# A two-layer hybrid encoder: the start of the program and the two token mixers rearranged

## The chip, the cores and the metric

The kernel runs on one core of one Trainium2 chip. The metric is the device time of one execution in microseconds. An execution of the kernel before takes 1383.24 us (median of three runs, 1381.23 to 1383.26). The five engines of the core are named as in the profile: PE is TensorE's matmul, PEld its weight load, DVE is VectorE, ACT is ScalarE, POOL is GpSimd, and SP is SyncE, which issues nearly all weight transfers here.

## The reference

A trunk of two layers over 256 tokens of width 1024, in fp32. Each layer has a token mixer and a channel mixer, each followed by a LayerNorm over the residual.

```python
def hybrid_mixer(x, ...):
    z = einsum('bsd,de->bse', x, w_in)
    cb, cc, ch, c_q, c_kv, k_r, lg, lx = split(z)
    y_conv = cb * dwconv3(cc * ch)                     # 256 channels
    y_mla  = mla(c_q, c_kv, k_r)                       # 8 heads of 64, low-rank q and kv
    y_lru  = griffin_recurrent(lg, lx)                 # 256 channels
    y = concatenate([rms_norm(y_conv), rms_norm(y_mla), rms_norm(y_lru)])
    return einsum('bse,ed->bsd', y, w_out)

def rglru_scan(x, w_a, b_a, w_i, b_i, lam, reverse):   # x: depthwise conv of 4 taps of lx
    rec = sigmoid(ga)                                  # ga, gi: block-diagonal products of x
    inp = sigmoid(gi)
    log_a = -8 * rec * softplus(-lam)
    a = exp(log_a)
    u = sqrt(-expm1(2 * log_a)) * (inp * x)
    h[t] = a[t] * h[t-1] + u[t]                        # forward, and backward with other weights
```

The first layer's channel mixer is a dense SwiGLU (3584 wide); the second's is eight SwiGLU experts of the same width, two of them for each token.

## The kernel before

The program is straight-line code in a schedule written by hand: each engine runs its instructions in the order in which the code emits them. The stages follow one another: the input LayerNorm with the transposes of x (`boundary(0)`, to about 28 us), mixer 0 (to about 125 us), `boundary(1)`, the dense channel mixer (150 to 380 us), `boundary(2)`, mixer 1 (391 to 492 us), `boundary(3)` with the router, and the experts (from about 512 us to the end).

Weights come as tiles of 1 MB (two pieces of 128 x 1024) through a ring of seven tiles. SP issues each transfer in one fixed order and waits there until the ring slot is free. `ahead` makes of a piece the two parts `hi` (rounded, by ACT at line 178 or, for the pieces in `HI_POOL`, by POOL at line 176) and `lo` (the rest, by DVE at line 185), some four pieces before `take` hands it to PE. A product of two such pairs is three matmuls (line 104). The first two pieces of a mixer are used raw, in fp32: their products go to `first` (line 330) as soon as parts of x are transposed (line 342) and copied out (lines 394, 396).

In a mixer PE runs the projections of x in the order `zq`, `zq`, gates, `zq`, gates, `zkv`, `zkv`, `zkr`, then eight `filler` groups and the attention of eight heads in between. `scores(h)` (line 750), `flip(h)` (the transposes at line 776) and `values(h)` (line 790) are PE's part of a head; DVE's `nm` (line 753) and `normalise` (line 768) stand between scores and flip. `values(h)` multiplies 64 columns of v with the transposed probabilities into one half (64 partitions) of a PSUM bank `po`, which two heads share.

The recurrence: DVE forms the convolution `xc` by four taps of two halves (lines 512, 514); `gates(d)` multiplies it on PE (line 552), ACT takes two Tanh, the second with the decay `cdec` as its scale; DVE's four reciprocals (line 575) and POOL's products make the decay and the input of the scan (lines 589, 591). That work is queued in `later`, and `tick()` emits the next item of it at chosen places. `cdec` is worked out of `lam` on 8 columns by `decay_consts` and `decay_rest`, mostly on DVE, in the middle of `boundary(0)`.

Of the kernel before, what the change touches and what calls it, by code (L numbers as in the profile page):

```python
# [10 lines left out]
F32 = mybir.dt.float32  # L11
# [20 lines left out]
PP_CONVW, PP_QG, PP_KVG, PP_LCW, PP_LCB = 0, 6, 9, 11, 19  # L32
HI_POOL = (1, 3, 5, 6, 7, 8, 10)
MIX_KINDS = [0] * 2 + [PIECE] * 2 + [0] + [PIECE] * 6 + [768] + [PIECE] * 2 + [768] + [PIECE] * 2 + [768] + [PIECE] * 2 + [768] + [PIECE] * 10
# [47 lines left out]
def hybrid_encoder_kernel(ctx, tc, x_in, pp_in, lnr_in, tab_in, wa_in, wm_in, out):  # L82
# [140 lines left out]
    for j in range(2):  # L223
        nc.sync.dma_start(out=rows0[:, j, 512:], in_=lnr_in[j:j + 1, 512:].to_broadcast([P, 512]))
        rows[0, j] = rows0[:, j, :]
    pp = consts.tile([P, PP_N], F32, name="pp")
# [44 lines left out]

    cdec = consts.tile([P, 8], F32, name="cdec")
    hbias = consts.tile([P, 2, 8], F32, name="hbias")

    def decay_consts():
        lam = consts.tile([P, 8], F32, name="lam")
        for l in range(2):
            o = l * PP_L
            G.tensor_scalar(lam[:, 4 * l:4 * l + 4], pp[:, o + PP_LAM:o + PP_LAM + 4], -1.0, 0.0, op0=OP.mult, op1=OP.add)
        na = consts.tile([P, 8], F32, name="nabs")  # L280
        G.tensor_scalar(na, lam, -1.0, 0.0, op0=OP.mult, op1=OP.add)
        V.tensor_tensor(na, na, lam, op=OP.min)
        t = consts.tile([P, 8], F32, name="texp")
        G.tensor_tensor(t, ebase.to_broadcast([P, 8]), na, op=OP.pow)
        return lam, t

    def decay_rest(lam, t):
        for l in range(2):
            V.tensor_scalar_mul(hbias[:, l, :], pp[:, l * PP_L + PP_BA:l * PP_L + PP_BA + 8], 0.5)
        s = consts.tile([P, 8], F32, name="sat")  # L290
        V.tensor_scalar_add(s, t, 2.0)
        V.reciprocal(s, s)
        V.tensor_tensor(s, s, t, op=OP.mult)
        z = consts.tile([P, 8], F32, name="zat")
        V.tensor_tensor(z, s, s, op=OP.mult)
        acc = consts.tile([P, 8], F32, name="accat")
        V.tensor_scalar_mul(acc, z, 1.0 / 17.0)
        for k in (15, 13, 11, 9, 7, 5, 3):
            V.scalar_tensor_tensor(acc, acc, 1.0 / k, z, op0=OP.add, op1=OP.mult)
        V.scalar_tensor_tensor(acc, acc, 1.0, s, op0=OP.add, op1=OP.mult)  # L300
        V.tensor_scalar(lam, lam, 0.0, 2.0, op0=OP.max, op1=OP.mult)
        V.scalar_tensor_tensor(cdec, acc, 4.0, lam, op0=OP.mult, op1=OP.add)

    def boundary(i, final=None, router=False):
# [63 lines left out]
        stats(0)  # L368
        if final is None:
            stats(1)  # L370
        x = xs[0][:, 512:]
# [5 lines left out]
        shift(0, 0, i)  # L377
        if final is not None:
            stats(1)
        if router:  # L380
# [24 lines left out]
        shift(1, 0, i)  # L405
        if i == 0:
            decay = decay_consts()
        centre(1, 1, i)
        shift(1, 1, i)
        if i == 0:  # L410
            decay_rest(*decay)
        if not router:
            for q in range(4):
                src, dh, dl = views(0, q)
                A.copy(dh, src)
                G.tensor_tensor(dl, y0[:, 2 * q:2 * q + 2], dh.bitcast(F32), op=OP.subtract)
            ahead(AHEAD, LOWS)
        if router:
# [42 lines left out]
    def mixer(l, xT, pz):  # L461
        o = l * PP_L

        def col(i):
            return pp[:, o + i:o + i + 1]

        with tc.tile_pool(name=f"mix{l}", bufs=1) as mx:
# [41 lines left out]
            A.copy(lxp[:, :, 1:S + 1], pz.rearrange("p (c t) -> p c t", c=2))  # L509
            for i in range(2):  # L510
# [35 lines left out]
            def gates(d, wgate):  # L546
                th = []
                for kind in range(2):
# [9 lines left out]
                    th.append(t)  # L558
                s = th[0]
                for i in range(2):  # L560
                    c = cdec[:, 4 * l + 2 * d + i:4 * l + 2 * d + i + 1]
                    A.activation(s[:, i * S:(i + 1) * S], s[:, i * S:(i + 1) * S], AF.Tanh, scale=c, bias=c)
                r = tmp("r")
                G.tensor_scalar(r, s, 1.0, 1.0, op0=OP.mult, op1=OP.add)
                V.tensor_scalar_max(s, s, 1e-30)
# [6 lines left out]
            def queue_recurrence():  # L572
                def inv(d, i):
                    sl = slice(i * S, (i + 1) * S)
                    V.reciprocal(rs[d][:, sl], rs[d][:, sl])

                def gate_input(d):
                    s, u, r = ss[d], us[d], rs[d]
                    V.scalar_tensor_tensor(u, u, 1.0, xc, op0=OP.add, op1=OP.mult)
                    G.tensor_tensor(s, s, r, op=OP.mult)  # L580
                    G.tensor_tensor(u, u, s, op=OP.mult)
                    G.tensor_scalar(r, r, 2.0, -1.0, op0=OP.mult, op1=OP.add)

# [14 lines left out]
                for d in range(2):  # L598
                    for i in range(2):
                        later.append(lambda d=d, i=i: inv(d, i))  # L600
                    later.append(lambda d=d: gate_input(d))
# [7 lines left out]
            def filler(i, between=None):  # L609
# [24 lines left out]
                elif i == 7:  # L634
                    gl["cb"] = tmp("cb")
                    A.copy(gl["cb"], pz)
                    G.tensor_tensor(gl["yc"], gl["yc"], gl["cb"], op=OP.mult)
                elif i == 5:
                    gx2 = tmp("gx2")
                    A.activation(gx2, pz, AF.Square)  # L640
                    gh = tmp("gh")
                    A.activation(gh, pz, AF.Copy, scale=0.5)
# [42 lines left out]

            rq = rms_scale(qsq, 384, "q")
            rkv = rms_scale(kvsq, 256, "kv")
# [93 lines left out]

            yms, msq, po = [], [], [None]

            def values(h):
                k = h % 2
                if k == 0:
                    po[0] = bank("po")
                pT = pTs.pop(h)
                for j in range(NB):
                    T.matmul(po[0][64 * k:64 * k + 64, 0:S], lhsT=vt[:, j, h * 64:(h + 1) * 64],  # L790
                             rhs=pT[:, j * S:(j + 1) * S], start=j == 0, stop=j == NB - 1,
                             skip_group_check=True)
                if k == 1:
                    yms.append(scaled_pair("ym", po[0][:, 0:S], col(PP_MG + 2 + h // 2), msq))

# [712 lines left out]
```

## Time and profile before

| | |
|---|---|
| runs, median of 3 | 1383.24 us |
| profiled execution, its own time | 1380.96 us |
| its span, first to last instruction | 1379.3 us |
| PE busy | 1343.9 us, 97% |
| DVE, ACT, POOL busy | 840.6, 671.6, 173.0 us |
| mean granted TensorE clock | 0.995 |

The profiled execution is 2.28 us shorter than the median of the runs. Its span is 1.66 us shorter than its own time. PE's busy time counts a matmul to its modelled end, so that overlapping matmuls leave no hole; what PE waits for stands in the view of waits.

### The profile page before, as it was taken

The page shows a single profiled execution, that of the slowest core. Times are in us where ns is not written, and L with a number is a line of the kernel's source. Part 1 is how long each engine was busy: PE and PEld are TensorE (multiplying, and loading weights), DVE is VectorE, ACT ScalarE, POOL GpSimd, SP SyncE. Part 2 cuts the span into 40 slices and gives each one's busy share as a digit, 9 for nine tenths or more (in the row PEclk, how much of TensorE's full clock was granted, in tenths as well). Part 3 has the DMA queues.
Part 4 walks back from the last instruction along what each step waited for, and adds up shares of the span by engine and source line. Part 5 has one row for each costly group of instructions (what it writes and reads, how often), then busy time and mean ns, then how long its engine had stood idle before and what let it go on. Part 6 is the DMA issues. An engine that isn't in the chain of part 4 may idle for free. (4 is left out here: it accounts for less than half of the span.)

```text
span 1379.3 us, 18986 instructions
## 1 busy us (share of the span) xinstructions
PE 1343.9 (97%) x7199; PEld 966.6 (70%) x7199; DVE 840.6 (61%) x1019; ACT 671.6 (49%) x954; POOL 173.0 (13%) x169
## 2 busy tenths in 40 slices
PE   6999999999999999999999999999999999999995
PEld 5987999999998883556665556666655666655674
DVE  7886644444589771455654555655645656544896
ACT  3763544444355621455444445554445545444674
POOL 4623311111164320000000000000000000000011
PEclk9999999999999999999999999999999999999998
DMA  8442655555074357999999999999999999999980
GB/s 324 165 179 92 228 200 184 184 184 183 31 287 151 159 208 303 421 421 421 420 421 421 421 421 421 421 421 421 420 421 421 421 421 421 421 421 409 419 356 33
DMA packets 61735, 437.73 MB, mean 317 GB/s; under 512 B 6850, under 2 KB 6978, under 8 KB 9284
## 3 DMA queue, kind: packets, MB, share of 16 engines
q1 hardware_dynamic: 60484, 432.25, 77.4%
q0 software_dynamic: 1152, 4.19, 0.9%
q8 instruction: 58, 0.95, 0.3%
q14 instruction: 41, 0.34, 0.1%
HBM read 435.37 MB, written 1.05 MB: 316 GB/s over the span
## 5 line engine op out<-in xcount | busy, mean ns | idle before, releaser
L185 DVE TENSOR_TENSOR lo<-w,hi 128x1024 fp32r<-128x1024 f32 (+1 forms) x474 | 571.1, 1244 | 55.4 <-ACT hi L178 53.3
L178 ACT CAST hi<-w 128x1024 fp32r<-128x1024 f32 (+1 forms) x462 | 471.5, 1046 | 140.8 <-DMA w<-in_wm_dram 57.0
L104 PE MATMUL gu<-hi,xg 128*128 128x512 f32 x896 | 295.6, 399 | 0.0
L1200 PE MATMUL gu<-w,xgl 128*64 128x512 f32 x896 | 205.3, 596 | 0.0
L104 PEld LDWEIGHTS gu<-hi,xg 128*128 128x128 f32 x896 | 168.6, 188 | 42.5 <-ACT hi L178 2.0
L104 PE MATMUL gu<-lo,xg 128*128 128x512 f32 x448 | 176.9, 395 | 0.2 <-DVE lo L185 0.2
L104 PE MATMUL py<-hi,hT 128*128 128x512 f32 x448 | 147.7, 400 | 0.0
L1200 PEld LDWEIGHTS gu<-w,xgl 128*64 128x64 f32 x896 | 60.9, 137 | 112.0 <-issue 110.8
L1116 ACT CAST hT<-pht 128x512 fp32r<-128x512 f32 x28 | 16.4, 585 | 230.3 <-PE pht L1111 230.3
L104 PE MATMUL gu<-xT_hi,hi 128*128 128x256 f32 x432 | 122.2, 283 | 0.0
L104 PE MATMUL gu<-xT_lo,hi 128*128 128x256 f32 x432 | 122.1, 283 | 0.0
L104 PE MATMUL gu<-xT_hi,lo 128*128 128x256 f32 x432 | 122.0, 282 | 0.0
L104 PEld LDWEIGHTS py<-hi,hT 128*128 128x128 f32 x448 | 84.3, 188 | 34.4 <-ACT hi L178 13.8
L1125 PE MATMUL py<-w,hTl 128*64 128x512 f32 x448 | 102.2, 598 | 0.0
L104 PEld LDWEIGHTS gu<-lo,xg 128*128 128x128 f32 x448 | 84.5, 189 | 18.8 <-DVE lo L185 0.5
L1117 DVE TENSOR_TENSOR hT<-pht,hT 128x512 fp32r<-128x512 f32 x28 | 19.3, 691 | 126.3 <-ACT hT L1116 126.3
L104 PE MATMUL py<-lo,hT 128*128 128x512 f32 x224 | 89.3, 399 | 2.4 <-DVE lo L185 2.3
L1215 DVE TENSOR_TENSOR h<-h,gu 128x512 f32<-128x512 f32 x28 | 19.2, 686 | 105.8 <-PE gu L104 105.8
L104 PEld LDWEIGHTS gu<-xT_hi,hi 128*128 128x128 f32 x432 | 82.6, 191 | 1.2
L104 PEld LDWEIGHTS gu<-xT_lo,hi 128*128 128x128 f32 x432 | 82.6, 191 | 1.0
L104 PEld LDWEIGHTS gu<-xT_hi,lo 128*128 128x128 f32 x432 | 82.7, 191 | 0.0
L1279 POOL TENSOR_TENSOR xl<-acc,xh 128x1024 fp32r<-128x1024 f32 x2 | 5.8, 2896 | 556.1 <-ACT xh L1278 556.1
(333 smaller groups left out, 1765.9 us busy)
## 6 DMA issues: line engine op xcount, KB each, us to landing
w<-in_wm_dram SPq DMA_DIRECT2D x336, 1024.0 KB, 15.9
w<-in_wa_dram SPq DMA_DIRECT2D x73, 1024.0 KB, 4.8
lnrows<-in_lnr_dram POOLq DMA_DIRECT2D x6, 512.0 KB, 5.2
x<-in_x_dram SPq DMA_DIRECT2D x2, 512.0 KB, 4.0
rows<-in_lnr_dram POOLq DMA_DIRECT2D x2, 512.0 KB, 10.5
out_dram<-z SPq DMA_DIRECT2D x4, 256.0 KB, 2.8
tab<-in_tab_dram SPq DMA_DIRECT2D x2, 320.0 KB, 7.5
lnrows<-in_lnr_dram SPq DMA_DIRECT2D x2, 256.0 KB, 6.4
```

The costliest lines, as they stand in the source:

```text
L104: T.matmul(dst, lhsT=a, rhs=b, start=start and i == 0, stop=stop and i == len(terms) - 1, skip_group_check=True)
L178: A.copy(hi[:, :kind], src[:, :kind])
L185: V.tensor_tensor(*todo, op=OP.subtract)
L1116: A.copy(hT[:, 0, :], pt)
L1117: V.tensor_tensor(hT[:, 1, :], pt, hT[:, 0, :].bitcast(F32), op=OP.subtract)
L1125: T.matmul(py[0][k * CAP:(k + 1) * CAP, :], lhsT=hp[:, j * CAP:(j + 1) * CAP], rhs=w[:, sl], start=first and j == 0, stop=last and j == 3, ...
L1200: T.matmul(pb[i * CAP:(i + 1) * CAP, :], lhsT=self.unit.xg[:, c, :], rhs=w[:, k * 512:(k + 1) * 512], start=c == 0, stop=c == DC - 1, skip ...
L1215: V.tensor_tensor(self.h, self.h, self.pgu[1], op=OP.mult)
L1279: G.tensor_tensor(xl[:, b], acc[0][:, b], xh[:, b].bitcast(F32), op=OP.subtract)
```

## The change

- `boundary(0)`: the statistics of the second block of x come after the first block is centred and shifted; the first weight tile is asked for ahead of the constants in the code; `spin(4)` and `spin(6)` put ten products of ones into PE's queue around the first two products.
- The decay constants are worked out on POOL alone: a first part after the first block's `xT_lo`, the rest inside mixer 0.
- Each mixer: one of the two halves of `xc` is formed on POOL; the decay `a` comes from an ACT Exp with scale and bias `cneg` = -2 `cdec` in place of DVE's reciprocals; the three products of `gate_input` run on DVE; the gates stand between other pieces of PE's work, and the tick list is shorter by four items.
- `HI_POOL` loses pieces 3, 5 and 6 of each mixer, whose `hi` ACT makes now (piece 1 is raw).
- `values` runs two heads at once, their matmuls in turn.

```diff
-HI_POOL = (1, 3, 5, 6, 7, 8, 10)
+HI_POOL = (7, 8, 10)
...
+    ahead(1)
...
-    def decay_consts():
+    def decay_first():
...
+        G.tensor_scalar(s, t, 1.0, 2.0, op0=OP.mult, op1=OP.add)
+        G.tensor_tensor(s, s, mone.to_broadcast([P, 8]), op=OP.pow)
+        G.tensor_tensor(s, s, t, op=OP.mult)
+        return lam, s
...
-        for k in (15, 13, 11, 9, 7, 5, 3):
-            V.scalar_tensor_tensor(acc, acc, 1.0 / k, z, op0=OP.add, op1=OP.mult)
...
+        for k in (13, 11, 9, 7, 5, 3, 1):
+            G.tensor_tensor(acc, acc, z, op=OP.mult)
+            G.tensor_scalar(acc, acc, 1.0, 1.0 / k, op0=OP.mult, op1=OP.add)
...
+        G.tensor_scalar(cneg, cdec, -2.0, 0.0, op0=OP.mult, op1=OP.add)
...
         stats(0)
-        if final is None:
-            stats(1)
...
-        if final is not None:
-            stats(1)
+        stats(1)
...
-        if i == 0:
-            decay = decay_consts()
         centre(1, 1, i)
         shift(1, 1, i)
-        if i == 0:
-            decay_rest(*decay)
...
+            def lru_taps(i):
                 d = xc[:, i * S:(i + 1) * S]
+                if i == 1:
+                    s = tmp("tap", (P, S), tag="sq", bufs=5)
+                    G.tensor_scalar(d, lxp[:, i, 0:S], col(PP_LCW + i), col(PP_LCB + i), op0=OP.mult, op1=OP.add)
+                    for j in range(1, 4):
+                        G.tensor_scalar(s, lxp[:, i, j:j + S], col(PP_LCW + 2 * j + i), 0.0, op0=OP.mult, op1=OP.add)
+                        G.tensor_tensor(d, d, s, op=OP.add)
+                    return
...
-                s = th[0]
+                s, r = th[0], tmp("r")
                 for i in range(2):
...
+                    A.activation(r[:, sl], s[:, sl], AF.Exp, scale=c, bias=c)
+                    c = cdec[:, k:k + 1]
+                    A.activation(s[:, sl], s[:, sl], AF.Tanh, scale=c, bias=c)
...
-                def inv(d, i):
-                    sl = slice(i * S, (i + 1) * S)
-                    V.reciprocal(rs[d][:, sl], rs[d][:, sl])
...
-                    G.tensor_tensor(s, s, r, op=OP.mult)
-                    G.tensor_tensor(u, u, s, op=OP.mult)
-                    G.tensor_scalar(r, r, 2.0, -1.0, op0=OP.mult, op1=OP.add)
+                    V.scalar_tensor_tensor(s, r, 1.0, s, op0=OP.add, op1=OP.mult)
+                    V.tensor_tensor(u, u, s, op=OP.mult)
...
+            lru_taps(1)
+            while rest_of_decay:
+                rest_of_decay.pop()()
             zq(0)
+            lru_taps(0)
             zq(1)
             wgate = take()
+            zq(2)
             gates(0, wgate)
-            zq(2)
+            zkv(0)
             gates(1, wgate)
+            zkv(1)
...
             queue_recurrence()
-            zkv(0)
-            tick()
-            zkv(1)
-            tick()
+            rq = rms_scale(qsq, 384, "q")
...
             def values(h):
...
+                if h % 2 == 0:
+                    return
+                po = bank("po")
+                pair = [pTs.pop(h - 1), pTs.pop(h)]
                 for j in range(NB):
...
+                    for k, pT in enumerate(pair):
+                        g = (h - 1 + k) * 64
+                        T.matmul(po[64 * k:64 * k + 64, 0:S], lhsT=vt[:, j, g:g + 64],
...
+    spin(4)
     for j in range(2):
...
+    spin(6)
     xT = boundary(0)
```

What stands in the engines' rows now, at three places.

DVE at the end of `boundary(0)`, before: the shift of the second block of x, then the chain of the decay, then the copies out of the transposes that PE's next products need.

```order
L261 SCALAR_TENSOR_TENSOR x_80<-x_80,rstd,lnrows 128x512
L289 TENSOR_SCALAR hbias<-pp 128x8 x2
L291 TENSOR_SCALAR sat<-texp 128x8
...
L299 SCALAR_TENSOR_TENSOR accat<-accat,zat 128x8 x7
L300 SCALAR_TENSOR_TENSOR accat<-accat,sat 128x8
L301 TENSOR_SCALAR lam<-lam 128x8
L302 SCALAR_TENSOR_TENSOR cdec<-accat,lam 128x8
L396 COPY xTf_217<-xTp 128x256 x2
L366 TENSOR_TENSOR xT_lo<-xTp,xT_hi 128x2x128 x4
```

The same place on DVE in the changed kernel.

```order
L265 SCALAR_TENSOR_TENSOR x_80<-x_80,rstd,lnrows 128x512
L402 COPY xTf_218<-xTp 128x256 x2
L375 TENSOR_TENSOR xT_lo<-xTp,xT_hi 128x2x128 x4
L185 TENSOR_TENSOR lo<-w,hi 128x1024 x3
L506 SCALAR_TENSOR_TENSOR cq_338<-zq,pp,cq_338 128x256
```

Nothing of the decay stands between the shift and the copies any more.

POOL around the start of mixer 0, before: `xT_lo` of the first block, four `hi` pieces, and the sum of squares of two `zq`.

```order
L416 TENSOR_TENSOR xT_lo<-xTf_137,xT_hi 128x2x128 x4
L176 TENSOR_SCALAR hi<-w 128x1024
L506 MEMSET lxp 128x2
L507 MEMSET lxp 128x2x2
L176 TENSOR_SCALAR hi<-w 128x1024 x3
L490 TENSOR_TENSOR cq0sq<-cq0sq,cq1sq 128x256
```

The same place on POOL in the changed kernel, ten rows of the first part of the decay and eighteen of the rest left out.

```order
L418 TENSOR_TENSOR xT_lo<-xTf_154,xT_hi 128x2x128 x4
...
L512 MEMSET lxp 128x2
L513 MEMSET lxp 128x2x2
L521 TENSOR_SCALAR xc<-lxp,pp 128x256
L523 TENSOR_SCALAR tap<-lxp,pp 128x256
L524 TENSOR_TENSOR xc<-xc,tap 128x256
...
L299 TENSOR_TENSOR zat<-sat 128x8
...
L308 TENSOR_TENSOR cdec<-accat,lam 128x8
L309 TENSOR_SCALAR cneg<-cdec 128x8
L176 TENSOR_SCALAR hi<-w 128x1024
L496 TENSOR_TENSOR cq0sq<-cq0sq,cq1sq 128x256
```

Seven rows of taps and twenty-one of the decay stand ahead of POOL's first `hi`, which is that of piece 7, the weights of the second `zkv`.

PE in the attention of mixer 0, before: the products of one head's values follow each `filler` (here those of the first two heads).

```order
L104 MATMUL zf<-xT_hi,lo 128x256
L790 MATMUL po<-pT,vt 64x256 x2
L750 MATMUL ps<-kt,q 128x256 x2
L776 MATMUL pt<-ident,pe 128x128 x4
...
L790 MATMUL po<-pT,vt 64x256 x2
L750 MATMUL ps<-kt,q 128x256 x2
L776 MATMUL pt<-ident,pe 128x128 x4
```

The same place in the changed kernel, with the numbers of the buffers.

```order
L761 MATMUL ps_893<-kt_625,q_803 128x256 x2
L787 MATMUL pt_898<-ident_87,pe_848 128x128 x4
...
L803 MATMUL po_974<-pT_846,vt_698 64x256
L803 MATMUL po_974<-pT_903,vt_698 64x256
L803 MATMUL po_974<-pT_846,vt_698 64x256
L803 MATMUL po_974<-pT_903,vt_698 64x256
L761 MATMUL ps_984<-kt_625,q_805 128x256 x2
```

The first head's products have moved behind the second head's flip and alternate with the second head's.

## Rows read from the trace of the kernel before

**Rows 1.** Waits of PE, whole span: us in total, times, longest.

```profile
PE first L330 <- DVE xTf L396: 3.3, 1, 3.3
...
PE pt L776 <- DVE pe L768: 3.1, 2, 1.6
...
PE bc_q L457 <- POOL rrs_q L451: 1.5, 2, 0.8
PE first L330 <- DMA w<-in_wa_dram: 0.8, 1, 0.8
```

**Rows 2.** Windows: us, busy us by engine (PE, PEld, DVE, ACT, POOL), clock, DMA share, GB/s.

```profile
24.20:27.50 3.30, 3.30 (x17) 3.30 (x18) 3.30 (x7) 0.72 (x3) 0.00 (x0) 0.50 0.77 318
28.00:65.00 37.00, 36.23 (x276) 34.51 (x275) 29.28 (x39) 22.05 (x41) 19.93 (x15) 1.00 0.53 192
515.00:520.00 5.00, 5.00 (x30) 2.40 (x29) 1.12 (x4) 0.53 (x2) 0.00 (x0) 1.00 0.01 3
...
540.00:600.00 60.00, 59.94 (x274) 32.36 (x271) 26.52 (x25) 24.72 (x30) 0.00 (x0) 1.00 1.01 422
```

**Rows 3.** Timeline of PE: start us, us, line, operation, count [idle before, releaser].

```profile
12.22 2.05 PE L330 MATMUL first<-xTf,w 128*128 128x128 f32 x8 [0.82 <-DMA w<-in_wa_dram]
...
24.02 4.57 PE L330 MATMUL first<-xTf,w 128*128 128x128 f32 x24 [3.33 <-DVE xTf L396]
28.35 0.36 PE L104 MATMUL zq<-xT_hi,hi 128*128 128x256 f32 x1
...
43.40 0.28 PE L104 MATMUL zkv<-xT_hi,hi 128*128 128x256 f32 x1
...
382.02 1.16 PE L330 MATMUL first<-xTf,w 128*128 128x128 f32 x8 [0.24 <-ACT xTf L394]
...
391.51 0.36 PE L104 MATMUL zq<-xT_hi,hi 128*128 128x256 f32 x1
```

**Rows 4.** Timeline of DVE, `boundary(0)`.

```profile
19.29 3.86 DVE L299 SCALAR_TENSOR_TENSOR accat<-accat,zat 128x8 f32<-128x8 f32 x7
...
23.55 0.75 DVE L396 COPY xTf<-xTp 128x256 f32<-128x256 f32 x2
```

**Rows 5.** Timeline of ACT, start of mixer 0.

```profile
28.63 0.59 ACT L509 COPY lxp<-first 128x512 f32<-128x512 f32 x1 [3.71 <-PE first L330]
```

**Rows 6.** Timeline of POOL, `boundary(0)` and mixer 0.

```profile
13.88 0.21 POOL L281 TENSOR_SCALAR nabs<-lam 128x8 f32<-128x8 f32 x1
...
20.29 2.05 POOL L176 TENSOR_SCALAR hi<-w 128x1024 fp32r<-128x1024 f32 x2
...
47.22 1.78 POOL L490 TENSOR_TENSOR ckvsq<-ckvsq 128x256 f32<-128x256 f32 x1 [2.96 <-ACT ckvsq L530]
...
112.97 0.73 POOL L490 TENSOR_TENSOR ymsq<-ymsq 128x256 f32<-128x256 f32 x1 [0.95 <-ACT ymsq L498]
```

**Rows 7.** The page, costliest groups: line, engine, operation, count, busy us, mean ns.

```profile
L185 DVE TENSOR_TENSOR lo<-w,hi 128x1024 fp32r<-128x1024 f32 (+1 forms) x474 | 571.1, 1244 | 55.4 <-ACT hi L178 53.3
L178 ACT CAST hi<-w 128x1024 fp32r<-128x1024 f32 (+1 forms) x462 | 471.5, 1046 | 140.8 <-DMA w<-in_wm_dram 57.0
```

**Rows 8.** Timeline of PE, attention of mixer 0 and a light expert.

```profile
66.18 0.59 PE L750 MATMUL ps<-kt,q 128*128 128x256 f32 x2
...
78.12 1.08 PE L790 MATMUL po<-pT,vt 128*64 128x256 f32 x4
79.12 1.13 PE L750 MATMUL ps<-kt,q 128*128 128x256 f32 x4
...
117.67 0.66 PE L776 MATMUL pt<-ident,pe 128*128 128x128 f32 x4
...
535.30 3.60 PE L1125 MATMUL py<-w,hTl 128*64 128x512 f32 x16
```

**Rows 9.** Timeline of DVE, attention of mixer 0.

```profile
71.75 0.66 DVE L753 TENSOR_REDUCE nm<-ps 128x2 f32<-128x512 f32 x1
...
116.21 1.37 DVE L768 TENSOR_SCALAR pe<-pe,sm 128x256 f32<-128x256 f32 x2
```

More of the change, by code (lines that the diff above doesn't have):

```diff
@@ L215, in hybrid_encoder_kernel @@
         xs.append(t)
+    for j in range(2):
+        nc.sync.dma_start(out=rows0[:, j, 512:], in_=lnr_in[j:j + 1, 512:].to_broadcast([P, 512]))
+        rows[0, j] = rows0[:, j, :]
+    ahead(1)
     def load_rows(i, eng=nc.gpsimd):
@@ L221, in load_rows @@
             eng.dma_start(out=rows[i, j], in_=lnr_in[2 * i + j:2 * i + j + 1, :].to_broadcast([P, D]))
-    for j in range(2):
-        nc.sync.dma_start(out=rows0[:, j, 512:], in_=lnr_in[j:j + 1, 512:].to_broadcast([P, 512]))
-        rows[0, j] = rows0[:, j, :]
     pp = consts.tile([P, PP_N], F32, name="pp")
@@ L234, in hybrid_encoder_kernel @@
     G.memset(ebase, float(np.e))
+    mone = consts.tile([P, 1], F32, name="mone")
+    G.memset(mone, -1.0)
     stat = {}
@@ L272, in hybrid_encoder_kernel @@
     cdec = consts.tile([P, 8], F32, name="cdec")
+    cneg = consts.tile([P, 8], F32, name="cneg")
     hbias = consts.tile([P, 2, 8], F32, name="hbias")
-    def decay_consts():
+    def decay_first():
         lam = consts.tile([P, 8], F32, name="lam")
@@ L279, in decay_consts @@
             G.tensor_scalar(lam[:, 4 * l:4 * l + 4], pp[:, o + PP_LAM:o + PP_LAM + 4], -1.0, 0.0, op0=OP.mult, op1=OP.add)
+            G.tensor_scalar(hbias[:, l, :], pp[:, o + PP_BA:o + PP_BA + 8], 0.5, 0.0, op0=OP.mult, op1=OP.add)
         na = consts.tile([P, 8], F32, name="nabs")
-        G.tensor_scalar(na, lam, -1.0, 0.0, op0=OP.mult, op1=OP.add)
-        V.tensor_tensor(na, na, lam, op=OP.min)
+        G.tensor_scalar(na, lam, 0.0, -2.0, op0=OP.max, op1=OP.mult)
+        G.tensor_tensor(na, na, lam, op=OP.add)
@@ L283, in decay_consts @@
         t = consts.tile([P, 8], F32, name="texp")
         G.tensor_tensor(t, ebase.to_broadcast([P, 8]), na, op=OP.pow)
[L285 to L289, printed above, removed]
         s = consts.tile([P, 8], F32, name="sat")
-        V.tensor_scalar_add(s, t, 2.0)
-        V.reciprocal(s, s)
-        V.tensor_tensor(s, s, t, op=OP.mult)
+        G.tensor_scalar(s, t, 1.0, 2.0, op0=OP.mult, op1=OP.add)
@@ L294, in decay_rest @@
+        G.tensor_tensor(s, s, mone.to_broadcast([P, 8]), op=OP.pow)
+        G.tensor_tensor(s, s, t, op=OP.mult)
+        return lam, s
+    def decay_rest(lam, s):
         z = consts.tile([P, 8], F32, name="zat")
-        V.tensor_tensor(z, s, s, op=OP.mult)
+        G.tensor_tensor(z, s, s, op=OP.mult)
         acc = consts.tile([P, 8], F32, name="accat")
-        V.tensor_scalar_mul(acc, z, 1.0 / 17.0)
-        for k in (15, 13, 11, 9, 7, 5, 3):
-            V.scalar_tensor_tensor(acc, acc, 1.0 / k, z, op0=OP.add, op1=OP.mult)
@@ L300, in decay_rest @@
-        V.scalar_tensor_tensor(acc, acc, 1.0, s, op0=OP.add, op1=OP.mult)
-        V.tensor_scalar(lam, lam, 0.0, 2.0, op0=OP.max, op1=OP.mult)
-        V.scalar_tensor_tensor(cdec, acc, 4.0, lam, op0=OP.mult, op1=OP.add)
+        G.tensor_scalar(acc, z, 1.0 / 17.0, 1.0 / 15.0, op0=OP.mult, op1=OP.add)
+        for k in (13, 11, 9, 7, 5, 3, 1):
+            G.tensor_tensor(acc, acc, z, op=OP.mult)
+            G.tensor_scalar(acc, acc, 1.0, 1.0 / k, op0=OP.mult, op1=OP.add)
+        G.tensor_tensor(acc, acc, s, op=OP.mult)
@@ L304, in boundary @@
+        G.tensor_scalar(lam, lam, 0.0, 2.0, op0=OP.max, op1=OP.mult)
+        G.tensor_scalar(acc, acc, 4.0, 0.0, op0=OP.mult, op1=OP.add)
+        G.tensor_tensor(cdec, acc, lam, op=OP.add)
+        G.tensor_scalar(cneg, cdec, -2.0, 0.0, op0=OP.mult, op1=OP.add)
+    rest_of_decay = []
     def boundary(i, final=None, router=False):
@@ L416, in boundary @@
                 G.tensor_tensor(dl, y0[:, 2 * q:2 * q + 2], dh.bitcast(F32), op=OP.subtract)
+            if i == 0:
+                decay = decay_first()
             ahead(AHEAD, LOWS)
@@ L438, in boundary @@
             keep(q)
+        if i == 0:
+            rest_of_decay.append(lambda: decay_rest(*decay))
         ahead(PIECES - 2, 2)
@@ L509, in mixer @@
             A.copy(lxp[:, :, 1:S + 1], pz.rearrange("p (c t) -> p c t", c=2))
-            for i in range(2):
+            def lru_taps(i):
                 d = xc[:, i * S:(i + 1) * S]
+                if i == 1:
[5 more added lines that the diff above has]
+                    return
                 V.tensor_scalar(d, lxp[:, i, 0:S], col(PP_LCW + i), col(PP_LCB + i), op0=OP.mult, op1=OP.add)
@@ L558, in gates @@
                     th.append(t)
-                s = th[0]
+                s, r = th[0], tmp("r")
                 for i in range(2):
[L561 to L564, printed above, removed]
+                    k = 4 * l + 2 * d + i
+                    sl = slice(i * S, (i + 1) * S)
+                    c = cneg[:, k:k + 1]
+                    A.activation(r[:, sl], s[:, sl], AF.Exp, scale=c, bias=c)
+                    c = cdec[:, k:k + 1]
+                    A.activation(s[:, sl], s[:, sl], AF.Tanh, scale=c, bias=c)
                 V.tensor_scalar_max(s, s, 1e-30)
@@ L598, in queue_recurrence @@
                 for d in range(2):
-                    for i in range(2):
-                        later.append(lambda d=d, i=i: inv(d, i))
                     later.append(lambda d=d: gate_input(d))
@@ L641, in filler @@
                     gh = tmp("gh")
-                    A.activation(gh, pz, AF.Copy, scale=0.5)
+                    A.activation(gh, pz, AF.Copy, scale=0.25)
                     G.tensor_scalar(gx2, gx2, 0.044715, 1.0, op0=OP.mult, op1=OP.add)
@@ L684, in keep_q @@
                     qs[h] = q
-            rq = rms_scale(qsq, 384, "q")
             rkv = rms_scale(kvsq, 256, "kv")
@@ L780, in flip @@
                 pTs[h] = pT
-            yms, msq, po = [], [], [None]
+            yms, msq = [], []
             def values(h):
[L785 to L788, printed above, removed]
+                if h % 2 == 0:
+                    return
+                po = bank("po")
+                pair = [pTs.pop(h - 1), pTs.pop(h)]
                 for j in range(NB):
[L790 to L794, printed above, removed]
+                    for k, pT in enumerate(pair):
+                        g = (h - 1 + k) * 64
+                        T.matmul(po[64 * k:64 * k + 64, 0:S], lhsT=vt[:, j, g:g + 64],
+                                 rhs=pT[:, j * S:(j + 1) * S], start=j == 0, stop=j == NB - 1,
+                                 skip_group_check=True)
+                yms.append(scaled_pair("ym", po[:, 0:S], col(PP_MG + 2 + h // 2), msq))
             acc = None
```

## The prediction, written before the run

> **What bounds the kernel now.** I begin with the view of PE's waits over the whole span [rows 1]. Its lines are all short: the longest single waits that this change touches are 3.3 us for DVE's copies in `boundary(0)`, 1.6 us for the first head's probabilities (once in each mixer), and 0.8 us for `rrs_q` (once in each mixer). So PE itself sets the end nearly everywhere, and a saving has to be one of those waits or PE's own work. The windows come second [rows 2]: from 540 us on both PE (59.94 of 60 us) and the transfers (share 1.01, 422 GB/s) are full, so whether the experts' stream hands on a gain made before it has to be asked. It ought to: at 515 to 520 us the stream stands nearly still (3 GB/s, share 0.01), because SP waits for ring slots that the program's progress frees. Its start, and with it the end, then moves with PE. The timelines come last; they give the prices.
>
> **The change, part by part.** I write T for the start of the first `zq`, 28.35 us before [rows 3].
>
> *The start.* PE's first raw product begins at 12.22 us after 0.82 us of waiting for the first weight tile [rows 3]. SP's rows keep their order in the changed kernel (small row, two blocks of x, two rows, tile, constants), so the earlier request in the code fetches nothing earlier, and the tile lands where it did. That part costs and gives nothing; the earlier first transposes end in the same wait. What changes comes after it. PE waits 3.33 us at 24.02 [rows 3] for copies that stand on DVE behind the chain of the decay: seven products of 8 columns took 3.86 us there, and the copies came at 23.55 [rows 4]. In the changed rows nothing of the decay stands ahead of them. From the first raw product to T it took 28.35 - 12.22 = 16.13 us. The same products at `boundary(2)` took 391.51 - 382.02 = 9.49 us [rows 3], at 2.4 GHz (mean granted clock 0.995 over the span) and with the small waits that such a boundary has. So the gain is 3.3 us (only the wait goes) to 6.6 us (the whole stretch runs like the later one). Which one depends on the clock: right after the 3.33 us wait the granted clock is 0.50, that is 1.2 GHz [rows 2]. In the changed kernel the spins keep PE at work to about 9 us (an estimate from their price below), then it waits some 3 us for the tile again, so they may or may not leave it at 2.4 GHz. I take the middle, 5.0.
>
> *The decay and the taps on POOL.* They stand ahead of POOL's `hi` of piece 7, on which the second `zkv` waits. `lxp` is copied at 28.63 + 0.59 = T + 0.87 [rows 5]. The seven taps are instructions of 128 x 256: 0.73 us for a product of two tensors when POOL is alone, 1.78 when DVE is in its way [rows 6]; the one-tensor ones are no dearer than 0.73. That is 7 x 0.73 = 5.1 us, at most 3 x 1.78 + 4 x 0.73 = 8.3. The 21 small ones of the decay: 0.21 us for the like [rows 6], 0.3 with issue (an estimate), 6.3 in all; at most DVE's price beside POOL's casts, 3.86 / 7 = 0.55 [rows 4], 11.6 in all. Then `hi`, 2.05 / 2 = 1.03 [rows 6], and `lo` on DVE, 1.24 [rows 7]. Piece 7 is ready at T + 0.87 + 5.1 + 6.3 + 1.03 + 1.24 = T + 14.5; in the bad case at T + 23.1. PE asks for it at 43.40 - 28.35 = T + 15.05 [rows 3], since the same pieces stand ahead of that group in the new order. So the wait is 0 to 8 us. I take 1.0, near the low end: DVE runs in order and stands at that `lo` itself while it is late, so it can't be in POOL's way then; the 1.0 covers the first part of the decay (two powers on POOL ahead of the taps) and Exp on ACT, which waits for `cneg` (T + 12.3 at best, when ACT comes to it). Behind a late Exp stand ACT's copies of `zkv`, whose squares the second RMS scale needs on PE.
>
> The Trainium skill (SBUF — State Buffer, "Who interferes with whom") speaks against this move: a GpSimd instruction and a VectorE instruction with two SBUF inputs share one port pair, and the second to come is blocked until the first has ended. The trace agrees, with 0.73 alone and 1.78 beside DVE [rows 6]. By that rule alone, with a `lo` in front of each of the 28 instructions, the sum would be that of the first rival below.
>
> *ACT.* It gets three `hi` casts of 1.05 us [rows 7] and four Exp of 128 x 256 in each mixer, each below the 0.59 of a 128 x 512 copy [rows 5]: some 5.5 us more in a stretch where it is busy 22.05 of 37 us [rows 2]. PE takes a piece about every 3 us and the casts run four pieces ahead, so I cost this at nothing; without that cover each late piece would cost its 1.05.
>
> *The recurrence.* Without reciprocals and with the scans earlier, DVE is on time for the first head. Before, `ps` began at 66.18 and takes 1.13 us [rows 8], but `nm` came at 71.75 [rows 9]: 4.4 us late, behind scans. That made the wait for `pe`, 3.1 us in two [rows 1]. It gives 0 to 3.1; I take 3.1, since the scans leave that place altogether. The earlier `rms_q` takes away the 1.5 us for `bc_q` [rows 1]: its power on POOL is now a whole group ahead.
>
> *Two heads at once.* One head's values take 79.12 - 78.12 = 1.00 us of PE for four records of 256 columns [rows 8], 2.00 for two heads. A light expert alternates two halves of a bank in the same way, on 64 columns of weights too: 16 records of 512 columns in 3.60 us, 0.225 each, where 256 columns alone cost 0.25 [rows 8]. So the two halves run side by side. Eight records of 256 columns are then 0.9 us, with a first and last without partner and the change of shape 1.15. That saves 0.85 a pair, 6.8 us for eight pairs. One saving is not kept: `normalise(7)` ends at 116.21 + 1.37 = 117.58 [rows 9] and its flip begins at 117.67 [rows 8]; PE will now be there 1.0 us earlier and wait 0.9, 1.8 in two mixers. Net 5.0; without overlap -1.8. The same price makes the ten spins of 512 columns at most 4.5 us at half speed, all ahead of 12.2.
>
> *The sum.* 5.0 - 1.0 + 3.1 + 1.5 + 5.0 = 13.6 us. From the profiled execution's own 1380.96 us this gives 1367.4; the median of the runs lies 2.28 above that execution, so the forecast is 1369.6.
>
> **The rivals.**
>
> *POOL's chain decides (slower).* Place: the 28 POOL instructions ahead of `hi` of piece 7. With a price p for each the wait of `zkv` is 0.87 + 28p + 2.27 - 15.05. Without a POOL wait the sum is a gain of 14.6, so the kernel gets slower from p = 0.95 us on. At p = 1.1 the wait is 18.9, and the time 1383.24 + 4.3 = 1387.5. For it: 1.78 us for one such product beside DVE [rows 6]. Against it: 0.21 for a small one [rows 6], and a DVE that stands waiting. 4 in 100.
>
> *The experts' stream takes the gain (no change).* If the transfers, full from 540 us on, and not PE set the end, and their start does not move, the time stays 1383.2. For it: the share of 1.01 [rows 2]. Against it: the idle stream at 515 us [rows 2], and no line of PE's waits names a weight transfer after the first tile. 5 in 100.
>
> *The two heads do not overlap.* The forecast without the 5.0 and with the 1.8 lost: 13.6 - 6.8 = 6.8, 1376.4. Against it: the light experts' rows [rows 8]; for it only that the two heads also have different weights, where the expert's two halves share theirs. 7 in 100.
>
> **How the numbers follow.** The forecast has 80 in 100, with 1365 to 1374 as its own range: the start can add 1.6 or take 1.7, POOL can give back 1.0 or take two or three more, DVE's lateness can stay in part, and runs of one kernel differ by 2 us. Another 4 in 100 go to several terms at their poor ends, 1374 to 1378. The range 1364 to 1376.5 takes in the first and most of the overlap rival. A measurement of this kernel can tell about 0.2%, 2.8 us, from no change: faster 0.91, same 0.05, slower 0.04.
>
> **What would show it.** In the changed profile the wait of `first` on DVE's copies is gone and the first `zq` begins near 23 us (21.7 at full clock, 25 without). POOL ends its `cneg` some 12 us after that, and the second `zkv` waits less than 2 us. The waits of `bc_q` and of the first `pt` are gone; a wait of about 0.9 us stands before the last flip of each mixer. Eight value records take 1.0 to 1.2 us. The experts begin some 13 us earlier and take as long as before. I would be wrong if small POOL instructions cost 0.5 us and more, if the value records stand 0.25 us apart, or if the experts' part grows by what the mixers save.

## The result and the profile after

The changed kernel takes 1363.95 us (median of four runs, 1363.19 to 1366.30), the kernel before beside it 1382.43 us. The ratio is 0.9874, 95% interval [0.9862, 0.9885]: faster by 18.5 us, where I had forecast 13.6 and a time of 1369.6. The profiled execution is the slowest of the four, with 1366.30 us and a span of 1364.5.

PE's waits in the changed kernel (us in total, times, longest). They answer to [rows 1].

```profile
PE zkv L104 <- DVE lo L185: 1.3, 1, 1.3
PE first L339 <- DMA w<-in_wa_dram: 1.3, 1, 1.3
...
PE pt L787 <- DVE pe L779: 1.2, 4, 0.3
...
PE zkv L104 <- POOL hi L176: 0.7, 1, 0.7
```

The 3.3 us behind DVE's copies and the wait of `bc_q` are gone, and what is left of `pt` is four short waits. The largest new ones are two waits of `zkv`, for POOL's `hi` and then for DVE's `lo` of piece 7; new too are two of 0.9 us in all for POOL's `yn` in the attention. PE's timeline at these places and at the marks of [rows 3, 8] (start, us, line, operation, count, idle before):

```profile
11.96 2.04 PE L339 MATMUL first<-xTf,w 128*128 128x128 f32 x8 [1.27 <-DMA w<-in_wa_dram]
...
17.70 1.06 PE L339 MATMUL first<-xTf,w 128*128 128x128 f32 x8
...
22.52 0.36 PE L104 MATMUL zq<-xT_hi,hi 128*128 128x256 f32 x1
...
38.44 0.39 PE L104 MATMUL zkv<-xT_hi,hi 128*128 128x256 f32 x1 [0.70 <-POOL hi L176]
...
40.22 0.57 PE L104 MATMUL zkv<-xT_hi,lo 128*128 128x256 f32 x1 [1.27 <-DVE lo L185]
...
102.70 1.08 PE L803 MATMUL po<-pT,vt 128*64 128x256 f32 x8
103.71 1.13 PE L761 MATMUL ps<-kt,q 128*128 128x256 f32 x4
...
108.74 0.30 PE L787 MATMUL pt<-ident,pe 128*128 128x128 f32 x1 [0.25 <-DVE pe L779]
109.38 0.55 PE L787 MATMUL pt<-ident,pe 128*128 128x128 f32 x3 [0.34 <-DVE pe L779]
...
520.40 3.60 PE L1137 MATMUL py<-w,hTl 128*64 128x512 f32 x16
```

The first `zq` stands 5.83 us earlier than in [rows 3], eight records of values take the 1.08 us that four took [rows 8], and the experts begin at 520.40, 14.9 us earlier. The windows around the waits of `zkv` (the last three numbers are granted clock, DMA share, GB/s) show what follows them:

```profile
38.00:40.20 2.20, 0.50 (x2) 0.30 (x2) 1.74 (x1) 2.13 (x6) 2.20 (x3) 1.00 0.00 0
40.30:43.60 3.30, 3.30 (x16) 3.30 (x17) 2.49 (x3) 3.23 (x9) 3.30 (x3) 0.50 0.75 226
```

After the second wait the clock is granted at 0.50, that is 1.2 GHz, and PE does 16 products in 3.3 us. POOL's timeline has the cause of the waits; ACT's and DVE's show what else stood behind `cneg` and behind that `hi`:

```profile
22.38 2.51 POOL L293 TENSOR_TENSOR sat<-sat,mone 128x8 f32<-128x8 f32 x1
...
25.82 0.56 POOL L521 TENSOR_SCALAR xc<-lxp,pp 128x256 f32<-128x256 f32 x1
...
29.82 0.79 POOL L524 TENSOR_TENSOR xc<-xc,tap 128x256 f32<-128x256 f32 x1
30.56 1.18 POOL L299 TENSOR_TENSOR zat<-sat 128x8 f32<-128x8 f32 x1
31.84 0.20 POOL L301 TENSOR_SCALAR accat<-zat 128x8 f32<-128x8 f32 x1
...
37.19 0.20 POOL L309 TENSOR_SCALAR cneg<-cdec 128x8 f32<-128x8 f32 x1
37.34 1.05 POOL L176 TENSOR_SCALAR hi<-w 128x1024 fp32r<-128x1024 f32 x1
```

```profile
37.42 0.60 ACT L578 ACTIVATE r<-th,cneg 128x256 f32<-128x256 f32 x1 [3.40 <-POOL cneg L309]
...
38.42 1.74 DVE L185 TENSOR_TENSOR lo<-w,hi 128x1024 fp32r<-128x1024 f32 x1 [6.34 <-POOL hi L176]
```

### The profile page after: what moved, and what is told of

It is laid out like the page before. It is cut to its first block, busy times and chain, and to the rows that moved or that the text cites. A ratio compares the mean times of both kernels' runs of the same rounds, so it can differ in the third digit from the quotient of the medians.

```text
span 1364.5 us, 19004 instructions
## 1 busy us (share of the span) xinstructions
PE 1337.7 (98%) x7209; PEld 965.6 (71%) x7209; DVE 822.6 (60%) x993; ACT 683.1 (50%) x969; POOL 166.9 (12%) x189
## 3 DMA queue, kind: packets, MB, share of 16 engines
HBM read 435.37 MB, written 1.05 MB: 320 GB/s over the span
## 5 line engine op out<-in xcount | busy, mean ns | idle before, releaser
L178 ACT CAST hi<-w 128x1024 fp32r<-128x1024 f32 (+1 forms) x468 | 477.9, 1047 | 132.4 <-PE gu L104 54.3
L104 PE MATMUL dacc<-hi,hp 128*128 128x512 f32 x224 | 74.1, 394 | 0.1
```

The source lines that it names most:

```text
L104: T.matmul(dst, lhsT=a, rhs=b, start=start and i == 0, stop=stop and i == len(terms) - 1, skip_group_check=True)
L178: A.copy(hi[:, :kind], src[:, :kind])
```

## The experiments

Theory: the gain is the sum of the prediction's terms, and POOL's chain gives part of it back. Rivals, term by term, stand in the expectations. Times are medians, ratios are to the kernel before, which took 1381.53 to 1381.83 us beside each group of four kernels. A profile is one execution of its kernel.

**The changed kernel again.**

> The changed kernel itself, once more, so that the experiments have it beside them. Theory: its profiled execution was 2.4 us above its other runs because GpSimd's chain was late by 2.0 us there (0.70 and 1.27 us of waits of the second zkv) and the granted clock fell to 0.50 for 3.4 us right after it, 1.7 us more; then another profile shows a time of 1363 to 1366.5 us together with a smaller or larger wait of zkv and with or without the clock's fall. Rival: the runs differ by 2 us for a reason elsewhere; then this profile has the same waits and the same fall of the clock at a time near 1364.

1363.27 us (1362.99 to 1363.97), ratio 0.9867 [0.9852, 0.9882]. Its profile has a span of 1361.3 us, 3.2 less than the first. One wait of `zkv` is left, 1.27 us, and the clock does not fall behind it (the windows first, then PE's start):

```profile
40.30:43.60 3.30, 3.30 (x30) 3.30 (x29) 3.20 (x4) 3.23 (x8) 2.75 (x3) 1.00 0.88 305
13.30:16.60 3.30, 3.30 (x19) 3.30 (x18) 1.48 (x3) 2.74 (x8) 1.65 (x3) 0.52 1.00 417
...
12.32 1.13 PE L339 MATMUL first<-xTf,w 128*128 128x128 f32 x8 [1.89 <-DMA w<-in_wa_dram]
...
22.41 0.36 PE L104 MATMUL zq<-xT_hi,hi 128*128 128x256 f32 x1
```

Thirty products where the first profile had 16. At `zkr` it is 2.2 us ahead (42.60 against 44.82), at the first `ps` 1.7, and near 570 us it gains another 1.5: there the first profile waited 0.77 and 0.33 us for a `lo`. So POOL's lateness and the clock's fall behind it make half of what that one execution had above the others, and the experts the other half; theory and rival each had a part. In this profile the clock fell near 13.4 us instead, 1.1 us after the end of a wait of 1.89 us for the tile; the first `zq` stands at 22.41 all the same.

**`hi` of pieces 7 and 8 on ACT.**

```diff
-HI_POOL = (7, 8, 10)
+HI_POOL = (10,)
```

> Only piece 10 keeps its hi on GpSimd; pieces 7 and 8 of each mixer get it from ScalarE. Theory (GpSimd's chain of taps and decay makes piece 7 late): the second zkv no longer waits 0.70 and 1.27 us in mixer 0, the clock stays at 1.0 there, and the profile is 2 to 3.7 us under that of the changed kernel; median 1361 to 1363 us. Rival (ScalarE has no room: its Exp waits for cneg to 37.4 us, and two more casts of 1.05 us stand in its queue): ScalarE's copies of zkv come later, rms_kv waits in place of zkv, and the time is 1363.5 to 1366.

1366.59 us, 0.9889 [0.9874, 0.9904]: the rival, 0.6 us above its range. The waits of `zkv` went, but POOL's chain became longer, for DVE now ran its `lo`s beside it. Rows of DVE, POOL, ACT, PE's waits and the windows of this kernel:

```profile
32.03 2.35 DVE L185 TENSOR_TENSOR lo<-w,hi 128x1024 fp32r<-128x1024 f32 x2
...
32.15 1.15 POOL L303 TENSOR_TENSOR accat<-accat,zat 128x8 f32<-128x8 f32 x1
33.39 1.05 POOL L304 TENSOR_SCALAR accat<-accat 128x8 f32<-128x8 f32 x1
34.53 0.20 POOL L303 TENSOR_TENSOR accat<-accat,zat 128x8 f32<-128x8 f32 x1
...
39.25 0.60 ACT L578 ACTIVATE r<-th,cneg 128x256 f32<-128x256 f32 x1 [5.24 <-POOL cneg L309]
...
PE rms_kv L452 <- POOL ckvsq L496: 4.1, 2, 3.7
...
47.00:53.50 6.50, 5.41 (x25) 5.42 (x26) 5.37 (x9) 4.45 (x6) 3.29 (x3) 0.50 0.90 347
```

Instructions of 128 x 8 cost 1.15 and 1.05 us beside DVE and 0.20 alone. Exp came 1.8 us later, ACT's copies of `zkv` behind it, and `rms_kv` waited 3.72 us; the clock fell in that wait, and the whole window of 6.5 us from 47.0 on is at 1.2 GHz.

**Products on ones up to the tile's arrival.**

```diff
             bring(0, 1, y0)
+            if i == 0:
+                spin(4)
             native(0, y0, (0,))
```

> Four more products on ones stand between the second transpose of x and the first raw product, where TensorE waits 1.27 us for the first weight tile. Theory (the clock rises to full speed 4.4 us after that wait because the wait broke TensorE's work): the rise comes at 13 to 15 us instead of 16.4, the first zq begins 0.7 to 1.7 us earlier, median 1362.5 to 1363.3. Rival (the rise does not hang on that wait): rise at 16.4, first zq at 22.5, or up to 0.5 us later because the products run past the tile's arrival; median 1364 to 1364.5.

1364.31 us, but from 1362.39 to 1369.68, 0.9887 [0.9867, 0.9908]: inconclusive as a time. The profiled execution, 1362.39, goes with the theory: the first products take 1.13 us from 11.78 on (2.04 in the first profile), and the first `zq` begins at 20.71:

```profile
11.78 1.13 PE L339 MATMUL first<-xTf,w 128*128 128x128 f32 x8
...
20.71 0.36 PE L104 MATMUL zq<-xT_hi,hi 128*128 128x256 f32 x1
```

Its waits of `zkv` are 0.72 and 1.28 us and the clock does not fall after them. The runs at 1369 have a mean clock of 0.991 against 0.996; where theirs fell, no profile shows.

**One head at a time.** The old `values` of the diff in the changed kernel.

> The values go one head at a time again; everything else as in the changed kernel. Theory (the two halves of the bank run side by side: 8 records in 1.15 us, not 2.0): 0.85 us a pair, 3.4 us in each mixer lost, less about 0.6 for the wait of the last flip in each mixer: 5.0 to 6.8 us slower, median 1369 to 1371. Rival (no overlap; what the attention gained came from the earlier scans): within 1 us of the changed kernel, 1363 to 1365.

1370.77 us, 0.9917 [0.9903, 0.9931]: the theory's time, though the 7.5 us to the repeated changed kernel are more than its 5.0 to 6.8. Between the first `pt` and `rms_m` the repeated changed kernel gains 3.6 us on the kernel before in each mixer. Without the pairs its lead stays where it was there (5.86 and 5.90 us, in mixer 1 9.01 and 9.09).

**Both halves of `xc` on DVE in mixer 0.**

```diff
-                if i == 1:
+                if i == 1 and l == 1:
```

> In mixer 0 alone both halves of xc are formed on VectorE again; GpSimd keeps the decay there, and its half of the taps in mixer 1. Theory (the second zkv waits because 5.1 us of taps stand ahead of the decay and of the hi of piece 7 on GpSimd): cneg ends near 31.5 to 32.5 us instead of 36.7 to 37.4, the two waits of zkv (0.70 and 1.27) go, VectorE has room for 2 us of taps where it waited 6.3; time 2.0 to 2.5 us under the changed kernel where its clock holds: 1361 us. Rival (VectorE's lo of pieces 4 and 5 come late behind the second half of the taps, and the gates wait for xc): waits of zq or pg of about 1.5 us in place of the old ones, 1362.5 to 1364.

1361.06 us, 0.9850 [0.9837, 0.9862], 2.2 under the changed kernel. The two intervals overlap, but all five runs (1359.62 to 1361.74) lie below the four of the repeated changed kernel. No wait of `zkv` is left, and none of `zq` or `pg` came. DVE's and POOL's rows of this kernel:

```profile
25.67 1.62 DVE L528 SCALAR_TENSOR_TENSOR xc<-lxp,pp,xc 128x256 f32<-128x256 f32 x3
...
35.18 1.75 DVE L185 TENSOR_TENSOR lo<-w,hi 128x1024 fp32r<-128x1024 f32 x1 [2.94 <-POOL hi L176]
...
30.86 1.06 POOL L303 TENSOR_TENSOR accat<-accat,zat 128x8 f32<-128x8 f32 x1
...
33.92 0.20 POOL L309 TENSOR_SCALAR cneg<-cdec 128x8 f32<-128x8 f32 x1
```

The `lo` of piece 7 starts at 35.18 us instead of 38.42. `cneg` ends 3.3 us earlier, not the five that I expected: beside the taps on DVE some of its steps cost 0.4 to 1.06 us.

**The decay on DVE again**, at its old place in `boundary(0)`.

> The decay constants are worked out on VectorE in the first boundary again (with cneg added); everything else as in the changed kernel. Theory (the start gained because nothing of the decay stands ahead of the copies of xTf): the wait of first for xTf is back with 2.5 to 3.5 us, the clock falls right after it as it did before the change, the first zq begins at 26 to 28 us; the waits of zkv (2.0 us) are gone, since GpSimd has only the taps. Net 1.5 to 4 us slower than the changed kernel: 1365 to 1367. Rival (the start gained from the spins and the clock): first zq at 22.5 to 24 and, without the waits of zkv, a time under the changed kernel, 1361 to 1363.

1364.61 us, 0.9875 [0.9860, 0.9889]. The time is too near the changed kernel's to tell; the rows are the theory's. The wait for `xTf` is back, and the clock falls with it:

```profile
21.53 2.71 PE L338 MATMUL first<-xTf,w 128*128 128x128 f32 x11 [2.85 <-DVE xTf L401]
...
21.60:24.70 3.10, 3.10 (x15) 3.10 (x16) 3.10 (x7) 0.83 (x3) 0.00 (x0) 0.53 1.02 425
```

The first `zq` begins at 25.64 (a little before the 26 to 28 expected), 3.2 us after the repeated changed kernel's, and the waits of `zkv` are gone. By the first `ps` only 0.8 of the 3.2 us is left. So between these two profiles moving the decay gives 3.2 us at the start and costs 2.4 behind it. The other 2.7 us of the start belong to the remaining edits there (the order of the statistics was not tried by itself). The share rests on one profile each, and the clock's fall near 13.4 us in the repeated one makes the 3.2 small: against the 20.75 of the next kernel, which starts as the changed one does and had no such fall, it is 4.9.

**The reciprocals again**, with the old `gate_input`, four items more in the list, two of them ahead of `rms_q`; then the same with those two behind it:

```diff
             queue_recurrence()
-            tick(2)
             rq = rms_scale(qsq, 384, "q")
+            tick(2)
```

> The recurrence goes as before the change: Tanh alone on ScalarE, r and three products on GpSimd, four reciprocals of 1.74 us on VectorE in each mixer, four more items in the list; the gates, the taps and the pairs of heads stay as in the changed kernel. Theory (without the reciprocals VectorE comes to the first head's nm in time): the 1.6 us wait of the first pt is back in both mixers, 3.1 to 4 us slower, 1366.5 to 1367.5. Rival (the earlier rms_q and the new order of the gates did that, not the reciprocals): under 1 us slower, 1363.3 to 1364.3.

> The recurrence with reciprocals, as in the run before with them, but the first two reciprocals (3.35 us) stand behind VectorE's rve of rms_q, not ahead of it. Theory (of the 10.5 us which the reciprocals cost there, 2.6 us were the wait of bc_q behind them, about 5 the clock's fall after that wait, and only the 1.5 to 1.7 us waits of the first pt come from the later scans): the waits of bc_q and the long stretch at 0.50 go, waits of pt stay, 1366.5 to 1368. Rival (the reciprocals are too long for this place wherever they stand): rve of rms_kv and bc_kv wait 2 us or more in its place, the clock falls all the same, 1370 to 1373.5.

1373.77 us, 0.9944 [0.9931, 0.9956], and 1373.17 us (1371.38 to 1377.28), 0.9936 [0.9923, 0.9950]: about 10 us slower in both. Of the first both sides had it wrong: the wait of the first `pt` came back with 1.54 us, in mixer 1 alone, and most was lost earlier, between the first `zf` and the first `ps` of mixer 0 (22.97 us against 15.51 in the repeated changed kernel). In the second my theory fell and its rival held. The start of the first, then DVE, PE and the windows of the second:

```profile
11.81 1.13 PE L339 MATMUL first<-xTf,w 128*128 128x128 f32 x8 [1.49 <-DMA w<-in_wa_dram]
...
20.75 0.36 PE L104 MATMUL zq<-xT_hi,hi 128*128 128x256 f32 x1
```

```profile
48.12 3.35 DVE L589 RECIPROCAL r<-r 128x256 f32<-128x256 f32 x2
...
52.53 0.14 DVE L455 TENSOR_SCALAR rve<-rms_kv 128x2 f32<-128x2 f32 x1
...
55.02 1.23 PE L463 MATMUL bc_kv<-ident,rrs_kv 128*128 128x128 f32 x4 [4.24 <-POOL rrs_kv L457]
...
53.30:59.90 6.60, 4.88 (x18) 4.01 (x19) 4.11 (x7) 2.01 (x4) 5.63 (x5) 0.51 0.46 160
494.00:507.40 13.40, 13.18 (x91) 11.29 (x90) 11.37 (x31) 3.93 (x8) 4.04 (x8) 1.00 0.78 314
507.50:514.20 6.70, 6.70 (x29) 5.35 (x30) 2.29 (x9) 0.99 (x4) 0.00 (x0) 0.50 0.01 2
```

Two reciprocals make a scale late in both places tried, PE waits 4.24 us for it (2.58 and 0.89 in the other order), and the clock falls. With the new order of the gates the Exp is needed. The profiled execution of the second is its slowest, 1377.28 us, and has a fall of the clock more: at 507.5 us, in the router, where PE had been busy 13.18 of 13.40 us and its longest wait was 0.20. What made it fall there no run shows.

**No products on ones**, in the changed kernel, and with both halves of `xc` on DVE in mixer 0.

> The ten products on ones at the start are left out; everything else as in the changed kernel. Theory (they run at half speed ahead of the tile's arrival and bring the clock's rise forward by little): the clock rises near 17.3 us, as before the change, not at 16.4, the first zq begins 0.4 to 0.6 us later, 1363.5 to 1364.3. Rival (they are what keeps the clock up after the wait for the tile, and so a large part of the 5.8 us of the start): rise past 19 us, first zq 2 to 3 us later, 1365.5 to 1366.5.

> Both halves of xc on VectorE in mixer 0, and no products on ones at the start. Theory (the spins bring the first zq forward by nothing, 22.2 against 22.4 to 22.5 us; what made the kernel without them 2.5 us slower in three runs of four was the clock's fall of 3.4 us after the waits of zkv, which are gone here): 1360.5 to 1361.7, as with the spins. Rival (the spins keep the clock up at the start): 1.5 us or more above the kernel with spins, 1362.5 to 1363.5.

1365.77 us (1363.48 to 1366.63), 0.9888 [0.9873, 0.9902], and 1361.73 us, 0.9857 [0.9842, 0.9872] against 1361.06 with them. The median of the first lies in the rival's range, but the profiled execution, its fastest (1363.48), goes with the theory:

```profile
22.22 0.36 PE L104 MATMUL zq<-xT_hi,hi 128*128 128x256 f32 x1
```

So a first `zq` near 22.4 doesn't need the ten products. That they bring it forward by nothing is more than the profiles show: of the seven profiles with these ten and the decay on POOL, six begin the first `zq` at 22.41 to 22.69 us, but the seventh, with the reciprocals, at 20.75, and there the first eight products took 1.13 us already. The second time is the theory's to 0.03 us. That the slower runs of the first had the clock's fall after `zkv` is argued from this; their records don't show where.

**The pairs of heads alone, in the kernel before.**

> The kernel before with one part of the change alone: the values of two heads at once. Theory (eight records side by side are a gain of TensorE's own time, whatever the other engines do): 3.5 us in each mixer, as the changed kernel loses without it (7.1 us from its profiles), so 1374 to 1375.5. Rival (VectorE is late for the heads there, so TensorE would only wait longer at the next flip): waits of pt grow by 2 us or more, gain of 3 to 5 us, 1376.5 to 1378.5.

1375.39 us, 0.9955 [0.9941, 0.9968]: 6.4 us faster. From the first `ps` to `rms_m` its profile gains 3.3 us, in mixer 1 3.4. The waits of `pt` grow from 3.1 to 4.3 us in all, so a late DVE takes little of it.

**The taps on DVE in mixer 0 and products up to the tile.**

> Both halves of xc on VectorE in mixer 0, and four more products on ones ahead of the first raw product. Theory (the two edits add: with the extra products the first zq began at 20.7 us instead of 22.4, and the runs at 1369 came from the waits of zkv, which are gone here): first zq near 20.8 us, no fall of the clock in the first 60 us, 1359 to 1360 us with a spread under 2.5 us. Rival (the extra products themselves make TensorE's clock fall in some runs): single runs at 1364 and above remain.

1360.00 us (1359.23 to 1360.34), 0.9840 [0.9827, 0.9854], the fastest of all, with no fall of the clock in the first 60 us and the first `zq` at 21.15. Its start, in PE's timeline:

```profile
10.34 2.04 PE L113 MATMUL spin<-ones 128*128 128x512 f32 x4
12.20 1.14 PE L339 MATMUL first<-xTf,w 128*128 128x128 f32 x8
```

All its runs lie below those of the repeated changed kernel. Its gain over the taps on DVE alone, 1.06 us, is inside the intervals.

## Why the prediction was right, and where its sizes were off

The sign and the mechanism of each term held. The forecast was 5.65 us too high: 1363.95 us is the very low end of the range of 1364 to 1376.5 (0.05 us under it), and below the 1365 to 1374 that I held likeliest. The sizes are what was off. The terms, read as differences of marks on PE between the profile of before and those of the changed kernel (us gained):

| term | forecast | first profile | repeated |
|---|---|---|---|
| start, to the first `zq` | 5.0 | 5.8 | 5.9 |
| POOL's chain, to the first `zf` | -1.0 | -4.0 | -2.0 |
| `bc_q`, first `zf` to first `ps`, both mixers | 1.5 | 2.5 | 2.1 |
| first `pt`, both mixers | 3.1 | 3.4 | 3.4 |
| pairs of heads, both mixers | 5.0 | 7.2 | 7.2 |
| elsewhere | 0 | -0.2 | 1.3 |
| sum | 13.6 | 14.7 | 17.9 |

The spans differ by 14.8 and 18.0 us, in agreement with the sums. That the first profile's sum comes within 1.1 us of the forecast is luck in part: POOL's chain cost 3.0 more than forecast, and the pairs, `bc_q` and the start gave 4.0 more.

- **Pairs of heads, the largest gain above the forecast.** The price of 0.85 us a pair was a little low: from the first record to the next `ps` eight records take 1.01 us (102.70 to 103.71) where four took 1.00, so a pair saves 0.99, 7.9 for eight and not 6.8. The 0.9 us wait before the last flip, 1.8 in two mixers, was too high: it is 0.25 and 0.34, 1.2 in both. DVE comes to `normalise(7)` earlier too. Taking the pairs out costs 7.5 us, and alone they give 6.4, so the gain is PE's own. The Trainium skill (TensorEngine Tiling (Array Packing), "Key Properties") says that different tiles of the array work independently; the 1.08 us for eight records as for four agrees.
- **The start.** 5.9 instead of 5.0, inside the bounds 3.3 to 6.6. The decay's move is 3.2 of it. The spins took 2.08 and 2.93 us, 5.0 and not at most 4.5. I left open whether they keep the clock up: in six of seven profiles they move nothing at the first `zq`, in the seventh the start gained 7.6 us, over the bound. The tile's arrival was indeed untouched (PE's first raw product at 11.96 against 12.22).
- **POOL's chain, undersized.** The taps took 4.8 us (5.1 forecast), the second part of the decay 6.8 (6.3). What failed in the sum is the term for what stands ahead of them, which was covered by the flat 1.0 us and not worked out: the first part of the decay, with a power of 2.51 us, keeps POOL to 25.67, so that the taps begin at T + 3.3 and not T + 0.87. `cneg` ends at T + 14.9, and the `lo` took 1.74 instead of 1.24. The waits are 1.97 us in one profile and 1.27 in the other, and PE waits 0.4 more for `ckvsq` at `rms_kv` in both. The clock's fall after them was in no term; it cost about 1.5 us in the first profile (14 products fewer in 3.3 us, 0.11 us each). The rival in which this chain decides had the right place; its price of 0.95 us for each instruction was reached by single ones only. The Trainium skill (SBUF — State Buffer, "Who interferes with whom") says that a VectorE instruction with two SBUF inputs contends with a GpSimd instruction that reads SBUF; the trace agrees, with 0.20 us for a small one alone and 1.15 beside a `lo`. What spared the sum was, as argued, that DVE stands waiting for that `hi` (6.34 us in the first profile); when ACT made the `hi` instead, the chain grew.
- **The recurrence.** 5.5 to 5.9 us for `bc_q` and `pt` together, forecast 4.6. The forecast priced the reciprocals by the old waits; in the new order they would have cost 10.
- **The experts' stream** passed the gain on: 14.9 us at their start, 14.75 at the end of the first profile, 16.6 and 18.0 in the repeated one. The 1.0 us that both gain on the kernel before between the tenth and the thirtieth group of `py` touches no edit, and its cause stays open.
- **The offset.** I added 2.28 us because three runs of before had a median of 1383.24; in the later groups it was 1381.5 to 1381.8, so about 1.5 of the error is that (an estimate).

## What to carry to other kernels

Before work is moved to an idle engine, add up what already stands in that engine's queue ahead of the first waiter, not only the moved work: here the first part of the decay, not the taps, was what the sum lacked. Price a wait on TensorE with the clock that may fall after it, and look for it in the windows; the cure here was to shorten the chain at its cheapest link (seven instructions back to the engine that stood waiting anyway). Two products that fill 64 columns each belong side by side, and that gain adds to the others, while edits that share a queue, as Exp and the order of the gates do, can't be priced or undone one at a time.

## What the runs showed of the hardware

- TensorE's granted clock was 0.50 during or soon after waits of 1.89 us (once), of 0.70 and 1.27 close together (in one of the six profiles that have both), of 2.58 and 0.89 (once), and of 2.85, 3.33 [rows 1, 2], 3.72, 4.24 and 5.12 us. The stretch at 0.50 is 3.4 us for those up to 3.33, but 10.2 for the pair of 2.58 and 0.89, and 6.8 for the last three. Once it fell for 6.8 us where no wait was over 0.20. Waits of 0.70 and 1.27 were followed by a fall in one execution and by none in another, which alone is 1.5 us between two runs of one kernel.
- The record of the clock has no row ahead of the first rise, and the windows show such a stretch as 1.00. So the start is read from the products: in the first profile the first row, of 1.00, begins at 16.38 us, and eight products take 2.04 us ahead of it and 1.06 behind it, the price of the lower level without a row of 0.50. In the repeated one it begins at 10.04, and eight took 1.13 at once. With products on ones up to the tile's arrival it began at 10.67 and 12.23, and they took 1.13 and 1.14 us from the first on.
- A power on GpSimd over 128 x 8 took 1.67 us with e as the base and 2.51 with -1 as the exponent, in part beside DVE, where a product of that size takes 0.20 alone.
